# Plain fp32 products in place of split ones in a hyena layer's transforms

## The chip, the cores and the metric

One core of one Trainium2 chip. The metric is the device time of one execution in microseconds; less is better. TensorE is PE, VectorE is DVE, ScalarE is ACT, GpSimd is POOL and SyncE is SP.

## The reference

Two layers over 512 latent tokens of width 1024, with 256 context tokens in the first: attention with an MLP, then a hyena layer with an MLP, all in fp32. The part that matters here is the hyena mixer:

```python
def bidir_long_conv(u, hf, hb, skip):
    L = u.shape[1]
    kfull = jnp.concatenate([hf, jnp.zeros_like(hf[:1]), hb[:0:-1]], axis=0)
    K = jnp.fft.rfft(kfull, n=2 * L, axis=0)
    uf = u.astype(F32)
    U = jnp.fft.rfft(uf, n=2 * L, axis=1)
    y = jnp.fft.irfft(U * K[None], n=2 * L, axis=1)[:, :L]
    return (y + uf * skip.astype(F32)).astype(u.dtype)

def hyena_mixer(h, w_in, conv_w, conv_b, ..., skip, w_out):
    z = short_conv(h @ w_in, conv_w, conv_b)
    x1, x2, v = jnp.split(z, 3, axis=-1)
    hf, hb = hyena_filters(...)
    y = v
    for n, gate in enumerate((x1, x2)):
        y = gate * bidir_long_conv(y, hf[:, n], hb[:, n], skip[n])
    return y @ w_out
```

## The kernel before

PE can take fp32 data in a reduced form, fp32r. To keep the precision of fp32 the kernel writes an operand as a sum of two fp32r tiles, hi (ACT casts) and lo (DVE subtracts, line 172; weights at lines 125 and 126), and makes three products of the halves: hi x hi, hi x lo and lo x hi (`mm3`, lines 107 to 111).

The hyena layer works on four groups of 256 channels, c = 0 to 3. The transforms are products with tables of cosines and sines, Tf (forward) and Ti (back), which `load_tables` brings from DRAM. For each group:

- `conv1(c)` transposes v into u and calls `hyena_conv` with quarter true. There `spectrum` multiplies u by Tf (8 triples), and DVE adds the results (line 938) into tiles named ft0 and ft1, merges them into U (line 926), multiplies by the filter's spectrum K (line 1076, one product of it on POOL), and forms the sums E and O, again in tiles named ft0 and ft1. From these come P0 and P1, split.
- `gate1` multiplies P0 and P1 by Ti (8 triples); DVE multiplies by x1 into y1, which is split into u.
- `hyena_conv` with quarter false makes the second convolution from that u; E and O are split into P0 and P1 as they are. The result is called R2.
- `gate2` uses R2 as the stationary operand and Ti as the moving one (16 triples); DVE multiplies by x2, and y is split for the output projection.

A transform tile has one buffer (bufs=1): u, U, ft0, ft1, P0 and P1 each exist once, and a new tile of a name waits until the last reader of the old one is done. Projections of later groups (and parts of the output projection) are put in between by `fill(n)`, each 24 products of 512 columns on PE, or 6 to 12 for the output. In the program conv1(c + 1) stands right behind the second convolution of c, then come 4, 5 or 9 fills, and then gate2(c). A scheduler orders the instructions of each engine by that priority when it builds the program, and lets a later one go first where an earlier one isn't ready. The order is fixed then.

After the loop the output projection's last part keeps its split weights for both token halves in tiles of the transforms that are no longer needed (`kept`, an alias of names), and the next MLP's first weights are put into others (`wx`).

Of the kernel before, what the change touches and what calls it, by code (L numbers as in the profile page):

```python
# [9 lines left out]
F32 = mybir.dt.float32  # L10
F32R = mybir.dt.float32r
AF = mybir.ActivationFunctionType
ALU = mybir.AluOpType
AX = mybir.AxisListType
P = 128
# [54 lines left out]
class Kernel:  # L70
# [840 lines left out]
    def load_tables(self, pool, inverse):  # L911

        nc, src = self.nc, self.a["k_dft"]
        res = []
        for nm, sl in (("Tf", slice(0, 8)), ("Ti", slice(10, 22))) if inverse else (("Tf", slice(0, 10)),):
            n = sl.stop - sl.start
            t = Split(pool.tile([P, n, P], F32R, name=nm + "hi", bufs=1), pool.tile([P, n, P], F32R, name=nm + "lo", bufs=1))
            nc.gpsimd.dma_start(out=t.hi, in_=src[:, 0, sl])
            nc.gpsimd.dma_start(out=t.lo, in_=src[:, 1, sl])
            res.append(t)  # L920
        return res

    def merge(self, U, E, O, e0, e1):

# [7 lines left out]
    def spectrum(self, T, x, pool, U):  # L932

        nc = self.nc
        V = nc.vector
        tt = lambda o, x, y, op: V.tensor_tensor(out=o, in0=x, in1=y, op=op)
        res = []
        for par in range(2):  # L940
            ps = {}
            for r in (par + 2, par):
                ps[r] = self.sm()
                for i in range(2):
                    self.mm3(ps[r][:, 256 * i:256 * i + 256], T[:, 2 * r + i], x[:, r], True, True)
            b = pool.tile([P, 512], F32, name=("fcb", "fsb")[par], bufs=1)
            nc.scalar.copy(b, ps[par + 2])
            a = ps[par]
            o = pool.tile([P, 2, 512], F32, name=f"ft{par}", bufs=1)
            tt(o[:, 0], a, b, ALU.add)  # L950
            if par == 0:
                tt(o[:, 1], a, b, ALU.subtract)
            else:
                for h in range(2):
                    sl, dl = slice(256 * h, 256 * h + 256), slice(256 - 256 * h, 512 - 256 * h)
                    tt(o[:, 1, dl], a[:, sl], b[:, sl], ALU.subtract)
            res.append((o[:, 0], o[:, 1]))
        self.merge(U, *res, V, V)
# [112 lines left out]
    def hyena_conv(self, hp, T, u, K, quarter):  # L1071


        nc = self.nc
        V, G = nc.vector, nc.gpsimd
        tt = lambda e, o, x, y, op: e.tensor_tensor(out=o, in0=x, in1=y, op=op)  # L1076
        U = hp.tile([P, 8, 256], F32, name="U", bufs=1)
        self.spectrum(T, u, hp, U)
        c, s = slice(0, 4), slice(4, 8)
        t0 = hp.tile([P, 4, 256], F32, name="ft0", bufs=1)  # L1080
        t1 = hp.tile([P, 4, 256], F32, name="ft1", bufs=1)
        tt(G, t1, U[:, c], K[:, s], ALU.mult)
        tt(V, t0, U[:, s], K[:, s], ALU.mult)
        tt(V, U[:, s], U[:, s], K[:, c], ALU.mult)
        tt(V, U[:, c], U[:, c], K[:, c], ALU.mult)
        tt(V, U[:, c], U[:, c], t0, ALU.subtract)
        tt(V, U[:, s], U[:, s], t1, ALU.add)
        E = hp.tile([P, 4, 256], F32, name="ft0", bufs=1)
        O = hp.tile([P, 4, 256], F32, name="ft1", bufs=1)

        tt(V, E, U[:, 0:8:2], U[:, 1:8:2], ALU.add)
        res = []
        for i, X in enumerate((E, O)):
            if i:
                tt(V, O[:, 0:4:2], U[:, 0:8:4], U[:, 1:8:4], ALU.subtract)
                tt(V, O[:, 1], U[:, 7], U[:, 6], ALU.subtract)
                tt(V, O[:, 3], U[:, 2], U[:, 3], ALU.subtract)
            d = Split(hp.tile([P, 4, 256], F32R, name=f"P{i}hi", bufs=1), hp.tile([P, 4, 256], F32R, name=f"P{i}lo", bufs=1))
            if quarter:
                for b, op in enumerate((ALU.add, ALU.subtract)):  # L1100
                    t = hp.tile([P, 2, 256], F32, name="y1", bufs=3)
                    tt(V, t, X[:, 0:4:2], X[:, 1:4:2], op)
                    self.split_to(d[:, 2 * b:2 * b + 2], t)
            else:
                self.split_to(d, X)
            res.append(d)
        return res

    def hyena(self, h, zp, first, open_hp, kdram, gcol, finish):
        nc, a = self.nc, self.a  # L1110
# [39 lines left out]

        def conv1(c):

            u = Split(hp.tile([P, 4, 256], F32R, name="uhi", bufs=1), hp.tile([P, 4, 256], F32R, name="ulo", bufs=1))
            for o, ps in turned(c, "v"):
                self.split_to(u[:, o], ps)
            return self.hyena_conv(hp, Tf, u, load_k(0, c), True)

        def turn_x1(c):
# [4 lines left out]

        def gate1(c, R, x1):

            u = Split(hp.tile([P, 4, 256], F32R, name="uhi", bufs=1), hp.tile([P, 4, 256], F32R, name="ulo", bufs=1))
            for o in range(2):
                ps = self.sm()
                for b in range(2):
                    for i in range(2):  # L1170
                        self.mm3(ps[:, 256 * b:256 * b + 256], Ti[:, 6 * o + 3 * i + b], R[o][:, 2 * b + i], i == 0, i == 1)
                t = hp.tile([P, 2, 256], F32, name="y1", bufs=3)
                nc.vector.tensor_tensor(out=t, in0=ps.rearrange("p (t n) -> p t n", t=2), in1=x1[:, o:4:2], op=ALU.mult)
                self.split_to(u[:, o:4:2], t)
            return u

        def gate2(c, R):

            for m in range(2):
                ps = self.sm().rearrange("p (o b n) -> p o b n", o=2, b=2)  # L1180
                for o in range(2):
                    for n in range(4):
                        i, j = 6 * o + 3 * (n // 2), n % 2
                        self.mm3(ps[:, o], R[o][:, n, m * P:(m + 1) * P], Ti[:, i:i + 2 + j:1 + j], n == 0, n == 3)
                t = hp.tile([P, S], F32, name="y1", bufs=3)
                v = lambda ap: ap.rearrange("p (b o n) -> p o b n", o=2, b=2)
                nc.vector.tensor_tensor(out=v(t), in0=ps, in1=v(Z[c]["x2"][m]), op=ALU.mult)
                s = Split(hp.tile([P, S], F32R, name="yhi", bufs=4), hp.tile([P, S], F32R, name="ylo", bufs=4))
                self.split_to(s, t)
                Y[2 * c + m] = s  # L1190
# [11 lines left out]
        hp = open_hp()  # L1202
        Tf, Ti = self.load_tables(hp, True)
# [7 lines left out]
        for c in range(4):  # L1211
            u = gate1(c, R1, turn_x1(c))
# [8 lines left out]
        fill(99)  # L1221
        kept = [Alias(p, {"whi": (hi, b), "wlo": (lo, b)}) for p, hi, lo, b in (
            (zp, "zv", "zx1", 2), (zp, "zv", "zx1", 2), (hp, "fcb", "fsb", 1), (zp, "zx2", "zx2", 2),
            *((hp, f"{nm}hi", f"{nm}lo", 1) for nm in ("P0", "P1", "Tf")), (hp, "ft0", "ft1", 1))]
        return finish(lambda hf: wo(6, 8, hf, kept))


# [32 lines left out]
    def build(self):  # L1260
        tc, nc, a = self.tc, self.nc, self.a

        pool = lambda **kw: tc.tile_pool(reuse_waits="tile", **kw)
        with ExitStack() as es:
# [41 lines left out]
            op = op_es.enter_context(pool(name="op", bufs=5))  # L1306
# [17 lines left out]
            hp = hp_es.enter_context(pool(name="hp", bufs=1, side="right"))  # L1324
            np_es = E(ExitStack())
            wx = np_es.enter_context(pool(name="wx", bufs=2, side="right"))
# [12 lines left out]
            with pool(name="mlp", bufs=1) as mp:  # L1339
                with ExitStack() as bg_es:  # L1340
                    for g in range(4):
                        H = self.mlp_up(0, h, mp, g, () if g else first)
                        if g == 0:
# [3 lines left out]
                            T, = self.load_tables(fp, False)  # L1347
# [8 lines left out]
                wx = np_es.enter_context(pool(name="wx2", bufs=2, side="right"))  # L1356
# [9 lines left out]
            hy = []  # L1366
# [6 lines left out]
            def finish(proj):  # L1373
                h = self.new_h(hp)
                np_ = Parts(hy[0].tile([P, 8, 256], F32, name="U", bufs=1),
                            Alias(hy[0], {"nxr": ("y1", 3), "nu": ("y1", 3)}),
                            {"nacc": (0, 1), "ny": (2, 3), "nv": (4, 5), "nt": (6,), "nsq": (7, 6)})
                wx = (Alias(hy[0], {"whi": ("uhi", 1), "wlo": ("ulo", 1)}),
                      Alias(hy[0], {"whi": ("x1T", 1), "wlo": ("Kin", 1)}))
                return h, self.project_norm_project(  # L1380
                    proj, lambda hf: self.normT(np_, h, m1[4], m1[3], hf), h,
                    lambda: self.weight(a["mlp_w1"][1][:, 0:256], KD, 256, wx), 3)
# [20 lines left out]
def _r12(x):  # L1403

    u = np.ascontiguousarray(x, np.float32).view(np.uint32).astype(np.uint64)
    u = (u + 0x7FF + ((u >> 12) & 1)) >> 12 << 12
    return u.astype(np.uint32).view(np.float32)


def _tables():  # L1410
    t = {}
# [37 lines left out]
            tabs += [fn(ang(eo)), fn(ang(eo + 2)), -fn(ang(eo + 2))]  # L1449
    m = np.stack(tabs, 1).astype(np.float64)  # L1450
    hi = _r12(m.astype(np.float32))
    t["k_dft"] = np.ascontiguousarray(np.stack([hi, _r12((m - hi).astype(np.float32))], 1))

    tt = np.arange(S, dtype=np.float32)
    tn = tt / np.float32(S)
# [33 lines left out]
```

## Time and profile before

| | |
|---|---|
| median of 3 runs | 1602.5 us (1600.34 to 1606.98) |
| profiled execution, device time | 1603.73 us |
| its span on the core | 1601.9 us |
| PE busy | 1467.2 us, 92% |
| DVE busy | 1151.7 us, 72% |
| ACT busy | 720.7 us, 45% |
| POOL busy | 468.5 us, 29% |
| mean granted clock | 0.964 of 2.4 GHz |

The hyena layer's conv loop lies between about 929 and 1207 us of the span. A busy PE is an engine with a product in flight: the distance between the starts of two products tells what one costs in a row of them, the length of one also holds its way through the array. An idle time is put down to what ended it.

### The profile page before, as it was taken

To read this page: it belongs to the slowest core of one execution; us is meant where nothing else is said; L and a number is where in the kernel's file an instruction comes from. 1 tells how busy PE (TensorE), PEld (TensorE's weight loads), DVE (VectorE), ACT (ScalarE), POOL (GpSimd) and SP (SyncE) were. 2 spreads that over 40 slices of the span, in tenths; PEclk is the share of its full clock that TensorE was granted. 3 is DMA by queue.
4 is the path that set the end of the run, shared out by engine and by line. 5 is a ranking of instruction groups with operands and counts; after the bars stand their busy time and mean duration, and the time that the engine had idled before them with its cause. 6 is when DMAs were issued, how large, how long until landed. Compare 5 with 4: busy or idle time off the path is not lost. (4 is left out here: it accounts for less than half of the span.)

```text
span 1601.9 us, 20203 instructions
## 1 busy us (share of the span) xinstructions
PE 1467.2 (92%) x7628; PEld 1217.3 (76%) x7628; DVE 1151.7 (72%) x1603; ACT 720.7 (45%) x1172; POOL 468.5 (29%) x363
## 2 busy tenths in 40 slices
PE   7689899999899999999999987888798999999998
PEld 2356688888887777877889866777677888888898
DVE  2888899887678898999755668888977534344354
ACT  3534587666654344345334534444235423232242
POOL 0350235222320332323221475666564000000001
PEclk9889899999999999999999998998998999999999
DMA  7556200221356555655334332221313132332341
GB/s 296 200 163 221 55 1 19 58 52 48 119 177 230 178 175 169 205 173 170 99 112 158 114 110 79 79 79 41 105 53 119 53 105 80 105 105 82 102 132 53
DMA packets 134751, 187.40 MB, mean 117 GB/s; under 512 B 16616, under 2 KB 117741, under 8 KB 131582
## 3 DMA queue, kind: packets, MB, share of 16 engines
q1 hardware_dynamic: 131904, 173.31, 33.6%
q0 software_dynamic: 2016, 12.32, 2.3%
q8 instruction: 60, 0.98, 0.3%
q10 hardware_dynamic: 734, 0.48, 0.1%
q14 instruction: 37, 0.30, 0.1%
HBM read 172.98 MB, written 10.49 MB: 115 GB/s over the span
## 5 line engine op out<-in xcount | busy, mean ns | idle before, releaser
L125 ACT CAST whi<-wraw 128x1024 fp32r<-128x1024 f32 (+3 forms) x211 | 198.8, 949 | 374.3 <-PE sm L110 341.4
L126 DVE TENSOR_TENSOR wlo<-wraw,whi 128x1024 fp32r<-128x1024 f32 (+4 forms) x184 | 223.8, 1219 | 129.4 <-ACT whi L125 126.1
L111 PE MATMUL sm<-h_hi,wlo 128*128 128x512 f32 (+1 forms) x720 | 277.7, 387 | 6.5 <-DVE wlo L126 5.5
L109 PE MATMUL sm<-h_hi,whi 128*128 128x512 f32 (+1 forms) x720 | 279.3, 391 | 3.7 <-ACT h_hi L420 2.3
L110 PE MATMUL sm<-h_lo,whi 128*128 128x512 f32 (+1 forms) x720 | 278.4, 387 | 2.9 <-POOL h_lo L424 2.3
L111 PE MATMUL sm<-mHhi,wlo 128*128 128x512 f32 (+1 forms) x640 | 223.1, 349 | 3.1 <-DVE wlo L126 3.1
L109 PE MATMUL sm<-mHhi,whi 128*128 128x512 f32 (+1 forms) x640 | 225.2, 352 | 0.5 <-ACT mHhi L169 0.3
L110 PE MATMUL sm<-mHlo,whi 128*128 128x512 f32 (+1 forms) x640 | 222.9, 348 | 2.5 <-DVE mHlo L172 2.5
L835 DVE SCALAR_TENSOR_TENSOR xT<-sm,mod,xT 128x512 f32<-128x512 f32 (+1 forms) x136 | 83.7, 621 | 138.9 <-PE sm L111 138.9
L111 PEld LDWEIGHTS sm<-h_hi,wlo 128*128 128x128 f32 x720 | 137.9, 192 | 35.8 <-DVE wlo L126 8.5
L110 PEld LDWEIGHTS sm<-h_lo,whi 128*128 128x128 f32 x720 | 138.2, 192 | 31.9 <-POOL h_lo L424 4.6
L109 PEld LDWEIGHTS sm<-h_hi,whi 128*128 128x128 f32 x720 | 138.0, 193 | 32.2 <-issue 3.4
L111 PEld LDWEIGHTS sm<-mHhi,wlo 128*128 128x128 f32 x640 | 121.1, 189 | 19.5 <-DVE wlo L126 4.6
L110 PEld LDWEIGHTS sm<-mHlo,whi 128*128 128x128 f32 x640 | 121.2, 189 | 19.2 <-DVE mHlo L172 3.4
L109 PEld LDWEIGHTS sm<-mHhi,whi 128*128 128x128 f32 x640 | 121.3, 190 | 17.2 <-issue 1.4
L926 POOL TENSOR_TENSOR Kout<-kE,kO 128x512 f32<-128x512 f32 x32 | 52.1, 1654 | 262.9 <-ACT kO L1064 262.9
L1242 POOL TENSOR_TENSOR facc<-facc,fsq 128x256 f32<-128x256 f32 x12 | 9.5, 789 | 333.5 <-ACT fsq L1240 333.5
L639 POOL TENSOR_SCALAR prob<-prob,smx 128x768 f32<-128x768 f32 x64 | 60.1, 939 | 149.1 <-DVE smx L638 95.7
L370 DVE SCALAR_TENSOR_TENSOR modacc<-modw,silu,modacc 128x1024 f32<-128x1024 f32 x63 | 83.8, 1330 | 11.0 <-DMA modw<-in_w_mod 10.6
L169 ACT CAST mHhi<-ms 128x512 fp32r<-128x512 f32 x64 | 39.7, 620 | 83.8 <-DVE ms L875 83.6
L1124 POOL TENSOR_TENSOR zx<-zx,zt 128x384 f32<-128x384 f32 (+1 forms) x64 | 60.4, 964 | 38.2 <-ACT zt L1122 37.0
L637 ACT ACTIVATE prob<-big,smx,qry 128x768 f32<-128x768 f32 x64 | 63.7, 996 | 11.1 <-DVE smx L635 10.4
(500 smaller groups left out, 3319.5 us busy)
## 6 DMA issues: line engine op xcount, KB each, us to landing
wraw<-in_mlp_w SPq DMA_DIRECT2D x67, 1024.0 KB
modw<-in_w_mod SPq DMA_DIRECT2D x80, 512.0 KB
wraw<-in_h_w_in SPq DMA_DIRECT2D x12, 1024.0 KB
wm<-in_w_mod SPq DMA_DIRECT2D x8, 1024.0 KB
kd<-Kout POOLq DMA_DIRECT2D x8, 1024.0 KB, 5.0
Kin<-kd SPq DMA_DIRECT2D x8, 1024.0 KB
wraw<-in_a_w_in SPq DMA_DIRECT2D x5, 1024.0 KB
wraw<-in_a_w_out SPq DMA_DIRECT2D x9, 512.0 KB
```

What stands on the lines that cost most here:

```text
L109: mm(ps, w.hi, x.hi, start=first, stop=False)
L110: mm(ps, w.hi, x.lo, start=False, stop=False)
L111: mm(ps, w.lo, x.hi, start=False, stop=last)
L125: nc.scalar.copy(hi, r3)
L126: (lo_eng or nc.vector).tensor_tensor(out=lo, in0=r3, in1=f(hi), op=ALU.subtract)
L169: nc.scalar.copy(dst.hi, src)
L370: nc.vector.scalar_tensor_tensor(out=acc, in0=w, scalar=s, in1=acc, op0=ALU.mult, op1=ALU.add)
L637: nc.scalar.activation(out=p, in_=sf, func=AF.Exp, bias=sm[:, 1:2], scale=sc, accum_out=sm[:, 2:3])
L639: nc.gpsimd.tensor_scalar(out=p, in0=p, scalar1=sm[:, 3:4], scalar2=1.0, op0=ALU.mult, op1=ALU.mult)
L835: nc.vector.scalar_tensor_tensor(out=xt, in0=ps, scalar=gcol[:, d:d + 1], in1=xt, op0=ALU.mult, op1=ALU.add)
L926: tt = lambda e, o, x, y, op: e.tensor_tensor(out=o, in0=x, in1=y, op=op)
L1124: nc.gpsimd.tensor_tensor(out=t[:, o0:o0 + n], in0=t[:, o0:o0 + n], in1=b[:, i0:i0 + n], op=ALU.add)
```

## The change

The transforms of the hyena layer's convolutions no longer use split operands. The table gets a third, unsplit copy in DRAM; `load_tables(pool, True)` loads Tf and Ti from it as fp32 on SP's queue, while the filter's tables stay split and on POOL's. `spectrum`, `gate1` and `gate2` make one fp32 product where `mm3` made three. u is a copy, or DVE's product itself; with quarter true P0 and P1 are written by DVE's sums; with quarter false `hyena_conv` returns E and O themselves. The kept weights and the next weights get other tiles, kw0 to kw3 and wl among them, since P0lo, P1lo, Tflo and ulo are gone.

```diff
@@ load_tables
-        for nm, sl in (("Tf", slice(0, 8)), ("Ti", slice(10, 22))) if inverse else (("Tf", slice(0, 10)),):
-            n = sl.stop - sl.start
-            t = Split(pool.tile([P, n, P], F32R, name=nm + "hi", bufs=1), pool.tile([P, n, P], F32R, name=nm + "lo", bufs=1))
-            nc.gpsimd.dma_start(out=t.hi, in_=src[:, 0, sl])
-            nc.gpsimd.dma_start(out=t.lo, in_=src[:, 1, sl])
-            res.append(t)
-        return res
+        if inverse:
+            for nm, sl in (("Tf", slice(0, 8)), ("Ti", slice(10, 22))):
+                t = pool.tile([P, sl.stop - sl.start, P], F32, name=nm, bufs=1)
+                nc.sync.dma_start(out=t, in_=src[:, 2, sl])
+                res.append(t)
+            return res
...
@@ spectrum
-                    self.mm3(ps[r][:, 256 * i:256 * i + 256], T[:, 2 * r + i], x[:, r], True, True)
+                    nc.tensor.matmul(ps[r][:, 256 * i:256 * i + 256], T[:, 2 * r + i], x[:, r], start=True, stop=True)
@@ hyena_conv
-            d = Split(hp.tile([P, 4, 256], F32R, name=f"P{i}hi", bufs=1), hp.tile([P, 4, 256], F32R, name=f"P{i}lo", bufs=1))
             if quarter:
+                d = hp.tile([P, 4, 256], F32, name=f"P{i}", bufs=1)
                 for b, op in enumerate((ALU.add, ALU.subtract)):
-                    t = hp.tile([P, 2, 256], F32, name="y1", bufs=3)
-                    tt(V, t, X[:, 0:4:2], X[:, 1:4:2], op)
-                    self.split_to(d[:, 2 * b:2 * b + 2], t)
-            else:
-                self.split_to(d, X)
-            res.append(d)
+                    tt(V, d[:, 2 * b:2 * b + 2], X[:, 0:4:2], X[:, 1:4:2], op)
+                X = d
+            res.append(X)
@@ conv1
-            u = Split(hp.tile([P, 4, 256], F32R, name="uhi", bufs=1), hp.tile([P, 4, 256], F32R, name="ulo", bufs=1))
+            u = hp.tile([P, 4, 256], F32, name="u", bufs=1)
             for o, ps in turned(c, "v"):
-                self.split_to(u[:, o], ps)
+                nc.scalar.copy(u[:, o], ps)
@@ gate1
-            u = Split(hp.tile([P, 4, 256], F32R, name="uhi", bufs=1), hp.tile([P, 4, 256], F32R, name="ulo", bufs=1))
+            u = hp.tile([P, 4, 256], F32, name="u", bufs=1)
...
-                        self.mm3(ps[:, 256 * b:256 * b + 256], Ti[:, 6 * o + 3 * i + b], R[o][:, 2 * b + i], i == 0, i == 1)
-                t = hp.tile([P, 2, 256], F32, name="y1", bufs=3)
-                nc.vector.tensor_tensor(out=t, in0=ps.rearrange("p (t n) -> p t n", t=2), in1=x1[:, o:4:2], op=ALU.mult)
-                self.split_to(u[:, o:4:2], t)
+                        nc.tensor.matmul(ps[:, 256 * b:256 * b + 256], Ti[:, 6 * o + 3 * i + b], R[o][:, 2 * b + i],
+                                         start=(i == 0), stop=(i == 1))
+                nc.vector.tensor_tensor(out=u[:, o:4:2], in0=ps.rearrange("p (t n) -> p t n", t=2), in1=x1[:, o:4:2], op=ALU.mult)
@@ gate2
-                        self.mm3(ps[:, o], R[o][:, n, m * P:(m + 1) * P], Ti[:, i:i + 2 + j:1 + j], n == 0, n == 3)
+                        nc.tensor.matmul(ps[:, o], R[o][:, n, m * P:(m + 1) * P], Ti[:, i:i + 2 + j:1 + j],
+                                         start=(n == 0), stop=(n == 3))
@@ hyena
-            *((hp, f"{nm}hi", f"{nm}lo", 1) for nm in ("P0", "P1", "Tf")), (hp, "ft0", "ft1", 1))]
+            (hp, "P0", "P1", 1), (hp, "kw0", "kw1", 1), (hp, "kw2", "kw3", 1), (hp, "ft0", "ft1", 1))]
@@ finish
-                wx = (Alias(hy[0], {"whi": ("uhi", 1), "wlo": ("ulo", 1)}),
+                wx = (Alias(hy[0], {"whi": ("u", 1), "wlo": ("wl", 1)}),
@@ _tables
-    t["k_dft"] = np.ascontiguousarray(np.stack([hi, _r12((m - hi).astype(np.float32))], 1))
+    t["k_dft"] = np.ascontiguousarray(np.stack([hi, _r12((m - hi).astype(np.float32)), m.astype(np.float32)], 1))
```

## Rows read from the trace of the kernel before

**Rows 1.** Busy (x count) by stretch: length, PE, PEld, DVE, ACT, POOL; clock, DMA.

```profile
929.00:1019.30 90.30, 73.67 (x362) 63.20 (x361) 73.90 (x71) 37.08 (x55) 57.34 (x41) 0.87 0.24 83
...
1000.30:1019.30 19.00, 19.00 (x103) 16.55 (x102) 16.61 (x16) 9.33 (x13) 13.86 (x10) 0.94 0.17 56
1019.30:1064.60 45.30, 35.62 (x181) 30.16 (x180) 40.96 (x45) 18.65 (x30) 27.51 (x20) 0.92 0.27 93
1064.60:1091.30 26.70, 25.22 (x128) 21.21 (x127) 24.27 (x22) 11.39 (x16) 21.23 (x15) 0.95 0.23 79
1091.30:1129.10 37.80, 28.61 (x146) 24.76 (x145) 31.77 (x39) 15.21 (x26) 20.02 (x15) 0.86 0.13 42
1129.10:1156.70 27.60, 21.89 (x113) 18.15 (x111) 24.12 (x28) 9.77 (x17) 16.66 (x13) 0.94 0.36 115
1156.70:1198.30 41.60, 37.57 (x190) 31.40 (x190) 33.40 (x42) 15.53 (x27) 22.53 (x18) 1.00 0.17 51
```

**Rows 2.** PE's waits from 929 to 1207.1: us in total, times, longest.

```profile
PE sm L110 <- DVE ulo L172: 12.1, 4, 4.0
PE sm L109 <- ACT uhi L169: 6.9, 4, 2.8
PE sm L109 <- ACT P0hi L169: 6.3, 3, 2.6
PE sm L109 <- ACT P1hi L169: 5.9, 2, 4.1
PE sm L110 <- DVE P0lo L172: 5.7, 3, 4.5
```

**Rows 3.** Timeline of PE around L405: start, length, instruction.

```profile
905.61 0.28 PE L111 MATMUL sm<-h_hi,wlo 128*128 128x256 f32 x1
905.73 0.59 PE L405 MATMUL sm<-nacc,ones 128*128 128x256 f32 x2
906.16 0.59 PE L406 MATMUL sm<-nsq,ones 128*128 128x256 f32 x2
...
906.71 0.28 PE L110 MATMUL sm<-h_lo,whi 128*128 128x256 f32 x1
```

**Rows 4.** Busy time of line 172, of line 169, and group ylo, 929 to 1211.

```profile
929.00:1211.00 282.00, 39.53 (x48) 0.00 (x0) 0.91 0.23 76
...
929.00:1211.00 282.00, 32.07 (x48) 0.91 0.23 76
...
L172 DVE TENSOR_TENSOR ylo<-y,yhi 128x512 fp32r<-128x512 f32 x8 | 7.2, 927 | 1.6 <-ACT yhi L169 1.6
```

**Rows 5.** Timeline of DVE: the second spectral sums and a first spectrum sum.

```profile
996.85 3.44 DVE L1076 TENSOR_TENSOR ft<-U 128x1024 f32<-128x1024 f32 x4
...
1001.53 0.69 DVE L938 TENSOR_TENSOR ft<-sm,fcb 128x512 f32<-128x512 f32 x1
...
1061.18 3.43 DVE L1076 TENSOR_TENSOR ft<-U 128x1024 f32<-128x1024 f32 x4
...
1126.64 2.48 DVE L1076 TENSOR_TENSOR ft<-U 128x1024 f32<-128x1024 f32 x4
...
1195.84 2.48 DVE L1076 TENSOR_TENSOR ft<-U 128x1024 f32<-128x1024 f32 x4
```

**Rows 6.** gate2's products with Tilo by group: min/median/max ns, first and last start.

```profile
L110 PE MATMUL sm<-Tilo,P1hi x8: 283/284/284, 1009.9 to 1018.9; 128*128 128x256 f32 x8
...
L110 PE MATMUL sm<-Tilo,P1hi x8: 283/284/284, 1087.0 to 1090.9; 128*128 128x256 f32 x8
...
L110 PE MATMUL sm<-Tilo,P1hi x8: 274/284/416, 1148.5 to 1156.3; 128*128 128x256 f32 x8
...
L110 PE MATMUL sm<-Tilo,P1hi x8: 284/350/416, 1201.1 to 1206.7; 128*128 128x256 f32 x8
```

**Rows 7.** The chain that ended last, behind the last gate2: start, length.

```profile
1207.05 0.41 ACT P1hi L125
...
1208.99 6.07 DMA wraw<-in_mlp_w
```

More of the change, by code (lines that the diff above doesn't have):

```diff
@@ L914, in load_tables @@
         res = []
-        for nm, sl in (("Tf", slice(0, 8)), ("Ti", slice(10, 22))) if inverse else (("Tf", slice(0, 10)),):
-            n = sl.stop - sl.start
-            t = Split(pool.tile([P, n, P], F32R, name=nm + "hi", bufs=1), pool.tile([P, n, P], F32R, name=nm + "lo", bufs=1))
-            nc.gpsimd.dma_start(out=t.hi, in_=src[:, 0, sl])
-            nc.gpsimd.dma_start(out=t.lo, in_=src[:, 1, sl])
-            res.append(t)
-        return res
+        if inverse:
[4 more added lines that the diff above has]
+            return res
+        t = Split(pool.tile([P, 10, P], F32R, name="Tfhi", bufs=1), pool.tile([P, 10, P], F32R, name="Tflo", bufs=1))
+        nc.gpsimd.dma_start(out=t.hi, in_=src[:, 0, 0:10])
+        nc.gpsimd.dma_start(out=t.lo, in_=src[:, 1, 0:10])
+        return [t]
     def merge(self, U, E, O, e0, e1):
```

## The prediction

> **What bounds the kernel now.** I began with the page: PE is the busiest engine by far, so a change to products is priced on PE first. But the change touches only the hyena layer, whose conv loop is the dip of PE in the page's slices, so the next view is busy time by stretch, cut where each channel group's second inverse transform (gate2) ends and where its second spectral sums are ready [rows 1]. There PE is busy 73.7 + 35.6 + 25.2 + 28.6 + 21.9 + 37.6 us of 90.3 + 45.3 + 26.7 + 37.8 + 27.6 + 41.6: between 929 and 1198.3 us it is idle 46.7 us, and DVE, busy 228 us of 269, is as loaded as PE. This layer is a chain between the two. PE's waits there are nearly all for the halves of split operands: 12.1 us for ulo, 6.9 for uhi, 6.3 for P0hi, 5.9 for P1hi and 5.7 for P0lo [rows 2]. The reader is to see that the layer is bound by order, not by one engine. Outside the layer nothing changes.
>
> The timeline of DVE gives the chain's marks. The second spectral sums of group 0 end at 1000.3, of group 1 at 1064.6, of group 2 at 1129.1, of group 3 at 1198.3 (start plus length of the four sums), and the next group's first spectrum sum starts 1.2 us after the first of them, at 1001.53 [rows 5]. gate2, which reads those sums, ends on PE later: 1019.3, 1091.3, 1156.7, 1207.1 (last start of Tilo x P1 plus the following products) [rows 6]. So today the next conv1 runs on DVE for 19.0, 26.7 and 27.6 us while gate2 waits its turn on PE, behind projections which stand before it in the program: in those stretches PE is busy 19.0 of 19.0, 25.2 of 26.7 and 21.9 of 27.6 [rows 1].
>
> **Products.** An fp32r product of 256 columns starts 0.12 us after the one before (905.61 to 905.73), so a split triple takes 0.36. A plain fp32 product of the same shape is on the trace: the sums over partitions at L405 and L406. Each is two instructions, and the pair takes 0.43 (905.73 to 906.16); the fp32r product after L406 again gets its place 0.43 later, 0.12 before 906.71 [rows 3]. The layer has 64 spectrum, 32 gate1 and 64 gate2 triples, 160 of 256 columns: 160 x (0.43 - 0.36) = **11.2 us more PE work**, 2.8 per group. PE gets no cheaper by this change. The row fits streaming: 0.43 is four times 256 columns at 2.4 GHz, while the fp32r product's 0.12 is more than 256 / 2.4 = 0.107. The Trainium skill (FP8 and Floating Point Precision, "TensorE Precision Notes") says that true FP32 is four passes through the array against one in the reduced form; by that alone the ratio is 4/3 and the addition 160 x 0.12 = 19 us, an estimate. The row gives less, since fp32r at this width is not held by its columns, and the row decides.
>
> **Removed splits.** The subtractions of line 172 take 39.5 us of DVE in the layer, 7.2 of them for y, which stays: 32.3 go. Line 169 takes 32.1 us of ACT; the cast of y stays, u from PSUM becomes a plain copy of the same size, the rest goes, some two thirds [rows 4]. DVE gains 8 us per group. In the chain to the first spectral sums (1000.3 today) this is worth: about 2.3 us at the first spectrum (ulo is one of PE's waits there, but the slower spectrum follows), 2.6 for the P halves, 1.3 for u after gate1, 1.3 for the next u's halves that were slipped in: **7.5 us, so 992.8** [rows 4, 5].
>
> **Moved: a wait that appears.** With quarter false the sums are no longer copied into P0/P1; gate2 reads E and O themselves, which are the tiles ft0 and ft1 with one buffer each. The next conv1's first spectrum sums are written to ft0 and ft1 too. So this DVE work, now at 1001.53 for group 1, must wait until gate2 of the group before has ended. Behind it on DVE stands the whole next conv1, and gate1, conv2 follow. The overlap of 19 to 27 us seen above is gone. I sum the layer along that chain:
>
> - 992.8 for the first sums.
> - From a gate2's end to the next sums: today first sum to last is 1001.53 to 1064.6, 63.1 us. Out of it go the halves of R2's P1 (1.2), P (2.6), u after gate1 (1.3), the next u (1.4) and some 1.2 of ACT casts between; the wider products add 0.9; some weight subtractions move into the wait (2). That leaves 55, and 57 for the third, which has residual updates in it [rows 4, 5].
> - gate2 itself after the last sums: 16 products, 7.2.
> - Total 992.8 + 55 + 55 + 57 + 7.2 = 1167, plus the three waits d0 + d1 + d2. Today's last gate2 ends at 1207.1, so the change is neutral at d0 + d1 + d2 = **40 us**; today the three are 73 [rows 5, 6].
>
> The waits are set by what PE has left to do. d0: up to the first gate2's end PE has 73.7 us of work and 16.6 idle [rows 1]; the work grows by 3.4, the idle halves, as half of it was for lo halves: 1019.3 + 3.4 - 8.5 = 1014, d0 = 21. d1: 35.6 + 25.2 + 2.9 = 63.7 of work, plus 6 idle (11.2 today), less 55 under the chain: 15. d2: 28.6 + 21.9 + 2.9 = 53.4, plus 9 idle (14.9 today), less 55: 7.4. Sum 43, **3 us later** than today. The longer chain lets PE do its projections under it, so these waits shrink, but the last group has little left to fill (37.6 of 41.6 today, then some 40 of 57).
>
> **Smaller edits.** The tables are two loads of 1.3 MB together on SP's queue, where there were four of 2.6 MB on POOL's. Behind them on SP stand the layer's weight loads; the nearest row has a load of 1 MB on that queue at 6.07 us [rows 7], so weights could come up to 8 us later, of which the second weight buffer hides most: I take nothing, 3 us at worst. POOL loses four issues, off the path. In the tail the kept weights no longer reuse P1 and Tf: today the cast into P1 waits for gate2's end (1207.05), frees the raw weight, whose next load takes 6.07 us and holds ACT ahead of the next norm [rows 7]. With own tiles that starts earlier: 0 to 3.5, I take **2 us** gained. The larger table in DRAM costs nothing.
>
> Sum against the profiled execution: span 1601.9, device time 1603.7; 1603.7 + 3 - 2 = 1605. The median of the runs is 1602.5, 1.2 lower, so I say **1603**: no change that can be measured.
>
> **Rivals.** *The gain stays.* The waits on ft0 and ft1 cost nothing because gate2 slips into PE's gaps early, so that d0 + d1 + d2 is near 3 x 7.2. Then PE bounds up to 1198.3: 222.6 us of work, 10 more for the products, and 46.7 of idle less 27 (all of ulo and P0lo, half of the three hi waits), together 252 in place of 269: **17 us faster, 1585**. For it: those waits are the largest on PE [rows 2], and DVE loses 8 us per group. Against it: PE is busy through all three waits with work that stands earlier in the program [rows 1].
>
> *Slower.* The held ft0 and ft1 stop the next conv1 while PE clears projections, and under the chain PE does no more of them than today, because their weights are split late on DVE and POOL. Then the waits stay near 57, that is 40 + 17: **1620**. It decides at a sum of 48 (40 + 8). For it: PE is idle 9.7 us of 45.3 and 9.2 of 37.8 in the chain stretches today although projections are left [rows 1]. Against it: the removed 8 us per group on DVE make those splits earlier.
>
> *Dearer or cheaper products.* If a plain product took the place of four fp32r products, 4 x 0.12 = 0.48, PE would work another 160 x 0.05 = 8 us: 1611. If the plain product were run in one instruction at fp32r's 0.12 the change would save 160 x 0.24 = 38 us, 1565; L405 speaks against both [rows 3].
>
> **How the numbers follow.** About 0.5% (8 us) is what a measurement of this kernel can tell from no change. Chances: forecast 0.43, gain stays 0.26, slower 0.26, products 0.05 (0.04 dearer, 0.01 cheaper). Range 1585 to 1622: the first two rivals at their prices, 2 us of chain above the slower one, leaving out the one-pass case, waits as long as today's, and the outer half of each rival. Faster 0.27, same 0.43, slower 0.30; the dearer product lies at the edge and goes to slower.
>
> **What would show it.** Products: pairs at 0.43 in the spectrum, PE work in the layer up by 11 us; 0.48 would make the dearer rival right. Splits: no rows of line 172 but ylo and what remains of the filters, and no wait of PE for ulo. The wait: DVE's first spectrum sum of a group starts only after gate2 of the group before, with DVE idle ahead of it, released by PE; if conv1 still starts right after the sums, I misread the buffers. Chain: about 55 us from gate2's end to the next sums. The waits: 21, 15 and 7. If their sum is under 32 the kernel is faster, over 48 slower. The forecast falls most easily with d1 and d2, which rest on how PE's work is ordered, and the trace of before can't show the new order.

## The result, and the profile after

The kernel after takes 1613.3 us (median of 12 runs, 1606.16 to 1615.87) where the kernel before takes 1602.6 in the same comparison (12 runs, 1595.41 to 1608.66): a ratio of 1.0057, 95% interval 1.0039 to 1.0075. It is slower by 0.57%, some 10.7 us. The forecast was 1603 us and no change that can be measured.

I begin with busy time by stretch, cut at the layer's first and last mark on PE: the end of the first transposes of `zv`, and the end of the last gate2. The columns are start, end and length, then the busy time of PE, PEld, DVE, ACT and POOL, the granted clock, the DMA share and GB/s. Of the kernel before:

```profile
0.00:930.03 930.03, 858.44 (x4540) 696.60 (x4540) 731.77 (x1099) 477.42 (x800) 269.26 (x206) 0.97 0.43 139
930.03:1207.07 277.04, 229.32 (x1149) 195.35 (x1150) 234.49 (x246) 109.02 (x173) 168.55 (x122) 0.91 0.22 74
1207.07:1601.90 394.83, 379.42 (x1941) 325.34 (x1939) 185.42 (x258) 134.24 (x201) 30.70 (x36) 0.98 0.30 94
```

And of the kernel after:

```profile
0.00:922.33 922.33, 858.07 (x4540) 696.19 (x4540) 729.85 (x1099) 477.23 (x800) 268.43 (x201) 0.97 0.44 140
922.33:1210.45 288.12, 229.37 (x990) 190.13 (x990) 195.94 (x206) 89.09 (x142) 162.50 (x124) 0.91 0.21 70
1210.45:1604.40 393.95, 377.50 (x1940) 323.38 (x1939) 185.87 (x258) 134.02 (x201) 30.05 (x35) 0.98 0.29 94
```

The layer grew from 277.0 to 288.1 us, the tail (what follows it) shrank by 0.9. Together that is 10.2, nearly all of the 10.7. The two spans alone, 1601.9 and 1604.4, hide this: the profiled run of after is the fastest of its runs and reached the layer 7.7 us earlier with the same work (PE 858.4 and 858.1 us there), and no run here shows why. Within the layer DVE lost 38.6 us and ACT 19.9, and PE is as busy as before. So the 11 us are idle time of PE.

The marks of the chain, in the kernel after: PE's timeline (start, length, instruction) with a spectrum and the four gate2s, then DVE's with the four second spectral sums, the first spectrum sums of the next group, and what DVE did ahead of one of them (in brackets the idle time before an instruction, and who ended it).

```profile
968.36 3.62 PE L948 MATMUL sm<-u,Tf 128*128 128x256 f32 x16
...
998.92 7.07 PE L1183 MATMUL sm<-Ti,ft 128*128 128x256 f32 x32
...
1071.96 7.07 PE L1183 MATMUL sm<-Ti,ft 128*128 128x256 f32 x32
...
1143.19 7.07 PE L1183 MATMUL sm<-Ti,ft 128*128 128x256 f32 x32
...
1203.30 7.15 PE L1183 MATMUL sm<-Ti,ft 128*128 128x256 f32 x32 [2.22 <-DVE ft L1079]
```

```profile
984.89 6.50 DVE L1079 TENSOR_TENSOR ft<-U 128x1024 f32<-128x1024 f32 x4
...
1004.62 1.28 DVE L941 TENSOR_TENSOR ft<-sm,fcb 128x512 f32<-128x512 f32 x2
...
1052.50 6.49 DVE L1079 TENSOR_TENSOR ft<-U 128x1024 f32<-128x1024 f32 x4
...
1067.58 1.43 DVE L126 TENSOR_TENSOR wlo<-wraw,whi 128x1024 fp32r<-128x1024 f32 x1 [7.24 <-ACT whi L125]
1075.68 0.69 DVE L1187 TENSOR_TENSOR y<-sm,zx 128x512 f32<-128x512 f32 x1 [6.68 <-PE sm L1183]
1077.06 0.69 DVE L172 TENSOR_TENSOR ylo<-y,yhi 128x512 fp32r<-128x512 f32 x1 [0.68 <-ACT yhi L169]
1077.67 1.28 DVE L941 TENSOR_TENSOR ft<-sm,fcb 128x512 f32<-128x512 f32 x2
...
1126.13 2.59 DVE L1079 TENSOR_TENSOR ft<-U 128x1024 f32<-128x1024 f32 x4
...
1200.83 3.59 DVE L1079 TENSOR_TENSOR ft<-U 128x1024 f32<-128x1024 f32 x4
```

The reader is to see the new wait. Before, the next group's first spectrum sum started right behind the last group's sums, at 1001.53 where the four end at 1000.3 [rows 5]. Now DVE's sums of group 1 end at 1059.0, gate2 of that group ends on PE at 1079.03, and the first spectrum sum of group 2 starts at 1077.67, as gate2 nears its end. In between DVE stood idle for 7.24 and 6.68 us. From sums to gate2's end the three waits are 14.6, 20.0 and 21.5 us. PE's waits in the layer (us in total, times, longest):

```profile
PE sm L1171 <- DVE P L1079: 43.8, 5, 16.2
PE sm L948 <- ACT u L1155: 7.0, 4, 3.4
PE sm L111 <- POOL wlo L126: 3.0, 2, 2.0
```

All waits for halves of transform operands [rows 2] are gone. In their place PE stands 43.8 us in five waits at gate1 (L1171) for P, which the end of conv1 writes. Two of the five, 5.0 us together, stand at group 0, ahead of any hold; the other three, 12.9, 16.2 and 9.6 us, wait for a conv1 that the held tiles delay. Here is a stretch by stretch view of the same kernel, cut at the marks. The last four rows are gate1's products of groups 1, 2 and 3 and one spectrum by themselves:

```profile
991.40:1005.99 14.59, 14.59 (x67) 12.46 (x66) 5.32 (x6) 7.18 (x10) 13.34 (x14) 1.00 0.44 144
1005.99:1059.00 53.01, 39.37 (x175) 32.74 (x175) 41.55 (x44) 15.85 (x24) 25.96 (x16) 0.87 0.17 60
1059.00:1079.03 20.03, 20.03 (x92) 16.91 (x92) 5.35 (x6) 8.23 (x11) 15.24 (x15) 1.00 0.20 65
1079.03:1128.70 49.67, 31.25 (x138) 26.03 (x137) 35.26 (x43) 12.04 (x21) 20.29 (x15) 0.83 0.14 48
1128.70:1150.25 21.55, 19.58 (x81) 16.09 (x80) 9.88 (x13) 6.87 (x13) 10.20 (x12) 0.92 0.35 107
...
1025.23:1030.67 5.44, 5.44 (x17) 4.49 (x18) 3.12 (x6) 0.00 (x0) 0.00 (x0) 0.67 0.01 3
1096.13:1101.96 5.83, 5.83 (x17) 4.81 (x18) 3.11 (x6) 0.00 (x0) 0.00 (x0) 0.63 0.00 0
1171.65:1177.26 5.61, 5.61 (x17) 4.67 (x18) 4.12 (x6) 0.00 (x0) 1.52 (x2) 0.65 0.01 3
968.36:971.98 3.62, 3.62 (x19) 3.16 (x18) 1.49 (x2) 3.62 (x6) 1.27 (x2) 1.00 0.07 9
```

DVE and PE now take turns. In the waits PE is full (20.03 of 20.03) and DVE nearly empty (5.35); under the chain DVE works (41.55 of 53.01) and PE idles 13.6 and 18.4 us. The idling costs a second time: after waits of 12.9, 16.2 and 9.6 us gate1's 16 instructions ran at a mean granted clock of 0.63 to 0.67, so partly at 1.2 and partly at 2.4 GHz. They took 5.44, 5.83 and 5.61 us, where the spectrum's 16 took 3.62 at a granted clock of 1.00.

### The profile page after: what moved, and what is told of

The parts are those of the page before. It is cut to its first block, busy times and chain, and to the rows that moved or that the text cites. A ratio compares the mean times of both kernels' runs of the same rounds, so it can differ in the third digit from the quotient of the medians.

```text
span 1604.4 us, 19790 instructions
## 1 busy us (share of the span) xinstructions
PE 1464.9 (91%) x7468; PEld 1209.7 (75%) x7468; DVE 1111.7 (69%) x1563; ACT 700.3 (44%) x1140; POOL 461.0 (29%) x359
## 5 line engine op out<-in xcount | busy, mean ns | idle before, releaser
L835 DVE SCALAR_TENSOR_TENSOR xT<-sm,mod,xT 128x512 f32<-128x512 f32 (+1 forms) x136 | 83.7, 621 | 149.8 <-PE sm L111 149.8
L111 PEld LDWEIGHTS sm<-mHhi,wlo 128*128 128x128 f32 x640 | 121.2, 189 | 19.9 <-DVE wlo L126 4.7
L1124 POOL TENSOR_TENSOR zx<-zx,zt 128x384 f32<-128x384 f32 x64 | 68.1, 1086 | 56.0 <-ACT zt L1122 54.7
L637 ACT ACTIVATE prob<-big,smx,qry 128x768 f32<-128x768 f32 x64 | 63.7, 996 | 11.5 <-DVE smx L635 10.9
```

Source lines behind the costliest of these rows:

```text
L111: mm(ps, w.lo, x.hi, start=False, stop=last)
L637: nc.scalar.activation(out=p, in_=sf, func=AF.Exp, bias=sm[:, 1:2], scale=sc, accum_out=sm[:, 2:3])
L835: nc.vector.scalar_tensor_tensor(out=xt, in0=ps, scalar=gcol[:, d:d + 1], in1=xt, op0=ALU.mult, op1=ALU.add)
L1124: nc.gpsimd.tensor_tensor(out=t[:, o0:o0 + n], in0=t[:, o0:o0 + n], in1=b[:, i0:i0 + n], op=ALU.add)
```

## The experiments

My theory after the result: the second sums held in `ft0` and `ft1` cost more than the removed splits bring, and the wider products cost their price on top. Rivals: the products alone make it slower; it is the order in which gate2 stands; or PE is held by the projections' own weight halves. All times are medians, all ratios against the kernel before, run beside each; a layer's length is from the one profiled run.

**e1_own.** The sums get tiles of their own.

```
-        E = hp.tile([P, 4, 256], F32, name="ft0", bufs=1)
-        O = hp.tile([P, 4, 256], F32, name="ft1", bufs=1)
+        E = hp.tile([P, 4, 256], F32, name="ft0" if quarter else "R20", bufs=1)
+        O = hp.tile([P, 4, 256], F32, name="ft1" if quarter else "R21", bufs=1)
```

> The changed kernel, but the second convolution's E and O (R2) get tiles of their own, R20 and R21, so that the next conv1 need not wait for gate2; the products stay plain fp32. Theory (the wait on ft0 and ft1 is what costs): the overlap of conv1 with gate2's wait comes back, the layer falls from 288 us to 255-265, the kernel to 1580-1592, below the kernel before; DVE's first spectrum sum starts within 2 us of the second spectral sums. Rival (dearer products cost it: 11 us more PE work, and the order doesn't matter): the kernel stays at 1608-1616.

Measured: 1596.2 us, ratio 0.9965 [0.9946, 0.9984]; the layer (from the same marks) 269.0 us. Nothing but two tile names turns the kernel after from 0.57% slower into 0.35% faster: 15 us by the ratios, 17 by the medians. The next conv1 starts right behind the sums again, as in the timeline of DVE:

```profile
983.57 6.60 DVE L1079 TENSOR_TENSOR R<-U 128x256 f32<-128x256 f32 x4
990.10 1.27 DVE L941 TENSOR_TENSOR ft<-sm,fcb 128x512 f32<-128x512 f32 x2
```

PE's waits, and POOL's timeline around the longest of them, which ends on PE at 1124.48:

```profile
PE sm L111 <- POOL wlo L126: 15.3, 3, 12.6
PE sm L111 <- DVE wlo L126: 7.3, 2, 3.9
PE sm L948 <- ACT u L1155: 7.2, 4, 3.4
PE sm L1171 <- DVE P L1079: 5.0, 2, 4.8
```

```profile
1113.76 3.38 POOL L1079 TENSOR_TENSOR ft<-U,Kin 128x1024 f32<-128x1024 f32 x1 [4.05 <-DVE U L929]
1117.10 5.66 POOL L1124 TENSOR_TENSOR zx<-zx,zt 128x384 f32<-128x384 f32 x4
1122.73 2.39 POOL L126 TENSOR_TENSOR wlo<-wraw,whi 128x256 fp32r<-128x256 f32 x2
```

The wait for P falls from 43.8 to 5.0 us. What is late next is a weight half of the output projection, queued on POOL behind a filter product and shifted sums: 12.6 us in one wait. POOL wasn't busy throughout: it stood idle for 4.05 us ahead of that filter product, which waited for DVE. I hadn't expected this wait, and I take it to be what holds the time above the expected 1592; no run shows that, as the three below that try to remove it get slower.

**e2_p.** The same with other tiles: the sums go to `P0` and `P1`, which are free then, so no memory is added.

```
+        E = hp.tile([P, 4, 256], F32, name="ft0" if quarter else "P0", bufs=1)
+        O = hp.tile([P, 4, 256], F32, name="ft1" if quarter else "P1", bufs=1)
```

> The changed kernel, but R2's E and O are written into P0 and P1, as the kernel before had R2's halves in P0 and P1: the next conv1 runs up to its own P and only there waits for gate2. Theory (the wait's place costs): nearly all of e1_own's gain, within 6 us of it, since gate2 ended before conv1 reached P in the kernel before. Rival (any hold by gate2 costs the same, wherever it stands): it stays with the changed kernel, 1608-1616.

Measured: 1595.4 us, 0.9957 [0.9937, 0.9977], layer 273.0 in the one profiled run: the same time as e1_own within the intervals. It isn't more memory that helps, but that the next conv1's first sums go to tiles that gate2 doesn't hold; only its last ones, into P0 and P1, must come behind gate2.

**e3_gate2first.** The other way to shorten the wait: gate2 ahead of the next conv1 and of the projections.

```
-            fill((0, 0, 1, 2)[c])
+            fill((2, 2, 2, 2)[c])
+            gate2(c, R2)
             if c < 3:
                 R1 = conv1(c + 1)
-            fill((4, 5, 9, 4)[c])
-            gate2(c, R2)
-            fill((1, 0, 2, 1)[c])
+            fill((3, 3, 10, 5)[c])
```

> The changed kernel with its shared ft0 and ft1, but gate2 stands in the program ahead of the next conv1 and of all projections except the two that make x2. Theory (the wait is long because gate2 stands behind 4, 5 and 9 projections on PE): the three waits d0+d1+d2 fall from 56 us to about 25, the chain from the first sums to the last gate2 falls by 20-30 us, and PE becomes the bound: 1585-1597. Rival (the waits are PE's own work and come back as idle PE later in the loop): 1605-1616.

Measured: 1632.1 us, 1.0177 [1.0152, 1.0202]. My expectation fell. gate2 came early, and PE then waited for the sums themselves:

```profile
PE sm L1183 <- DVE ft L1079: 31.3, 4, 10.4
PE sm L1171 <- DVE P L1079: 18.5, 7, 4.8
```

What I had called a wait was PE's own projections, and with gate2 ahead of them they were not done earlier either: each kind of projected tile has two buffers, which I take to be why, though that wasn't tried. The layer is 293.9 us and what follows it 405.9, where the kernel after has 288.1 and 394.0: PE's idle time in the layer grew from 58.8 to 66.0 us, and 12 of the 18 us by which the two together grew are products that now stand behind the loop (11.3 us more PE work there). So moving gate2 forward didn't remove the cost; part of it became a wait of PE, and this edit alone can't say how much of the rest is the moved work.

**e4_before_hold.** The hold without the plain products: the kernel before, with the hi halves of the second sums in `ft0` and `ft1`. The sums themselves, which had been there, go to `x1T` and a tile of their own, by two more lines that aren't shown.

```
+            d = Split(hp.tile([P, 4, 256], F32R, name=f"P{i}hi" if quarter else f"ft{i}", bufs=1),
+                      hp.tile([P, 4, 256], F32R, name=f"P{i}lo", bufs=1))
```

> The kernel before, split products and all, with the hold alone: the hi halves of R2 are put into ft0 and ft1, so that the next conv1 waits for gate2 as in the changed kernel; E is made in x1T and O in a tile of its own in its place. Theory: slower than the kernel before by 15-30 us, 1617-1632, with DVE idle ahead of the first spectrum sums. Rival (the hold is harmless, the products cost the 10 us): within 5 us of the kernel before.

Measured: 1631.4 us, 1.0167 [1.0138, 1.0195]. PE's waits:

```profile
PE sm L109 <- ACT P0hi L169: 38.6, 4, 16.3
PE sm L110 <- DVE ulo L172: 15.0, 4, 5.4
```

The hold alone costs 27 us by the ratio, 30 by the medians, on split products, with the same wait at gate1 (longest 16.3, in the kernel after 16.2). So a hold alone is enough for a loss; what the reuse of `x1T` adds to it wasn't run by itself. The kernel after lies some 18 us below this one (1.0167 less 1.0057). That isn't what the rest of the change is worth without a hold: e1_own is only some 6 us below the kernel before.

**e7_own_three and e8_own_one.** What the products themselves cost: e1_own with single fp32r operands and three equal fp32r products in each place, or one. Both leave out the low halves, and both load the tables on POOL's queue.

```
+    def mmr(self, ps, w, x, first, last):
+        for n in range(3):
+            self.nc.tensor.matmul(ps, w, x, start=first and n == 0, stop=last and n == 2)
```

> e1_own, but every operand of the transforms is one fp32r tile and every product is three equal fp32r products, which takes PE 0.36 us in place of 0.43; the lo halves and so part of each product are left out, and the tables come on POOL's queue. It has the split kernel's PE work without its splits. Theory (the dearer product is paid where PE is the bound, in the waits for gate2, but is partly hidden under the chain): faster than e1_own by 4-11 us. Rival (PE's idle time swallows it): within 4 us of e1_own.

> As e7_own_three, with one fp32r product where there were three: two thirds of each product are left out, 0.12 us of PE in place of 0.43, some 50 us less PE work in the layer. Theory (the layer is a chain of DVE, ACT and POOL steps with PE work under it): the kernel falls by much less than 50 us against e1_own, 15-30 us. Rival (PE is the bound of the layer once the hold is gone): 40-50 us.

Measured: 1583.3 us, 0.9881 [0.9848, 0.9915], and 1580.1 us, 0.9866 [0.983, 0.9901]. The layers by themselves, three products and one:

```profile
926.73:1181.58 254.85, 218.53 (x1149) 188.56 (x1150) 203.91 (x206) 89.16 (x143) 168.95 (x125) 0.93 0.23 79
```

```profile
929.22:1180.66 251.44, 195.35 (x829) 158.42 (x830) 206.27 (x203) 87.53 (x140) 163.64 (x123) 0.86 0.24 79
```

In e1_own PE is busy 228.9 us there with 990 instructions (I read it from the same view). Three reduced products in place of a plain one take 10.4 us off PE and 13 off the time, more than the 4 to 11 that I expected: with the hold gone the wider product seems to be paid. The next 23 us of PE's work bring 2 to 3, within the intervals of the two: there PE waits 19.1 us for P and 11.6 for u, so I take the chain to be the bound. I can't say how much of the 13 us is due to order: the POOL wait of 12.6 us in e1_own is 7.7 in e7_own_three.

**e6_own_dve, e11_own_alt and e9_before_dve.** Three tries at the late weight halves: the output projection's low halves on DVE in place of POOL, in e1_own and in the kernel before, and every second one in e1_own.

```
-            w_out, list(range(r0, r1)), gcol, lambda k: Y[r0 + k], cols, kept, (nc.gpsimd, nc.gpsimd))
+            w_out, list(range(r0, r1)), gcol, lambda k: Y[r0 + k], cols, kept, (nc.vector, nc.vector))
```

> e1_own with one more edit: the lo halves of the output projection's weights are subtracted on DVE instead of POOL. In e1_own PE waited 12.6 us in one piece for such a half, which stood on POOL behind the filter product and short-convolution sums. Theory (DVE's freed time is not yet used, and POOL's order holds PE): that wait goes, the kernel comes to 1582-1592, below e1_own. Rival (the next in line is as late, or DVE's chain pays for it): within 4 us of e1_own.

> The kernel after with own tiles for the second sums, and of the output projection's weights each second low half on DVE in place of POOL. With all of them on POOL the longest wait of PE is one of 12.6 us for such a half, with all on DVE there are 29.6 us of waits for them. Theory, that it is the place in the two queues that decides and no engine is free of it: half of them on each gives waits for low halves of 12 to 25 us in sum and a time between the two, 1597 to 1604. Rival, that POOL was only overloaded: the sum falls below 10 us and the time to 1586 to 1592.

> The kernel before with the edit of e6_own_dve alone (lo halves of the output projection's weights on DVE). Theory (there DVE is the loaded engine and has no room): same as the kernel before or slower, 1600-1610. Rival (the edit gains on its own, whatever the products): faster than the kernel before by 5 us or more.

Measured: 1605.1 us, 1.0019 [1.0002, 1.0037] for e6_own_dve; 1609.0, 1.0034 [1.0013, 1.0056] for e11_own_alt; 1613.1, 1.0073 [1.0049, 1.0098] for e9_before_dve. All three lie above the kernels that they were made from by 9 to 12 us by the ratios, and above what I expected. PE's waits in e6_own_dve, in e11_own_alt, then in e9_before_dve:

```profile
PE sm L111 <- DVE wlo L126: 29.6, 6, 8.4
```

```profile
PE sm L111 <- DVE wlo L126: 20.0, 5, 7.0
PE sm L111 <- POOL wlo L126: 11.3, 3, 7.7
```

```profile
PE sm L111 <- DVE wlo L126: 24.8, 5, 14.9
```

PE's waits for low halves from either queue come to 22.6 us in e1_own (15.3 and 7.3), 32.6 in e6_own_dve (with 3.0 from POOL) and 31.3 in e11_own_alt; in the kernel before they are 5.6, in e9_before_dve 25.6 (with 0.8 from POOL). So the half comes late in either queue: on POOL behind a filter product and shifted sums, on DVE, as I take it, behind the chain. That POOL was only overloaded is refuted, as half the load on each brought more waits than POOL's share alone. e1_own and e2_p stay the best of the full kernels.

**e10_after_nosums.** The kernel after without most of the shifted sums on POOL, for a thing seen in the marks: four sums that took 3.44 and 3.43 us before [rows 5] take 6.50 and 6.49.

```
-                    nc.gpsimd.tensor_tensor(out=t[:, o0:o0 + n], in0=t[:, o0:o0 + n], in1=b[:, i0:i0 + n], op=ALU.add)
+                    if n < 130:
+                        nc.gpsimd.tensor_tensor(out=t[:, o0:o0 + 1], in0=t[:, o0:o0 + 1], in1=b[:, i0:i0 + 1], op=ALU.add)
```

> The kernel after, of whose short convolution's shifted sums on POOL (L1124) the two 384 wide ones of each tile are left out and the other two cut to one element, so the filter is not computed in full. In the kernel after the four second spectral sums take 6.50 and 6.49 us on DVE in groups 0 and 1, while POOL runs L1124, where the kernel before has 3.44 and 3.43. Theory, that DVE runs slower beside a busy POOL: with L1124 gone the four sums take 2.5 us in both groups, the first of them are ready some 4 us earlier, 65 us after the layer's start in place of 69.1, and the layer is 274 to 282 us in place of 288. Rival, that the sums are slower for another reason (their inputs come late, or their form): they stay near 6.5 us and the layer near 288. The held tiles are still there, so in neither case does the time fall to that with own tiles: 1598 to 1607 by the theory, 1610 to 1615 by the rival.

Measured: 1594.5 us, 0.9954 [0.9929, 0.9978], layer 273.6. The sums:

```profile
979.69 4.58 DVE L1079 TENSOR_TENSOR ft<-U 128x1024 f32<-128x1024 f32 x4
```

They got shorter, but not 2.5: POOL was still at a weight half and two of the cut sums. The time fell further than either theory said, from 1613 to 1594.5, I think because the shifted sums also stand in the chain (the next gate reads their tiles), so this run doesn't price the slowed sums alone. The wait for P is still 35.0 us in four, so the hold is still there. The reader should see that the hold isn't the only lever: with it in place, leaving out work on POOL brought 16 us by the ratios, about what the tile names bring.

## Where the prediction was right and where it was wrong, step by step

The mechanism was right, and so was the side on which it decides: I wrote that over 48 us of waits the kernel is slower, and they are 56.2. The forecast of 43 was the step that failed, and in it the idle time that I left to PE in the periods of groups 1 and 2. The range, 1585 to 1622, holds the time; the largest chance, 0.43, stood on no change, and 0.30 on slower.

From the layer's start the terms compare so (start 930.03 before, 922.33 after):

- **First sums:** forecast 62.8 us (992.8 less 930.03), measured 69.1 (991.4 less 922.33), 70.3 before. Of the 7.5 us of splits only 1.2 came off. The second spectrum didn't follow gate1: it starts at 968.36, behind a projection of 24 products that PE runs from 961.6, so I take the removed halves of u to have been hidden there. And the four sums took 3 us longer. Not seen: PE's queue at that place. **+6.3.**
- **Chains from a gate2's end to the next sums:** forecast 55, 55 and 57, measured 53.0, 49.7 and 54.2. The terms that I listed for 55 add up to 54.3. **-10.2.**
- **Waits:** forecast 21, 15 and 7.4, measured 14.6, 20.0 and 21.5. **+13.2.** I had let PE's idle time shrink to 6 and 9 us in the periods of groups 1 and 2; it is 13.6 and 20.4 (the unfilled parts of the stretches above). PE's work was even a little less than I summed (59.4 and 50.8 us against 63.7 and 53.4). What I missed is where the idling comes from: gate1 of the next group stands on PE ahead of the remaining projections, and PE stops there for P. This is the rival *slower*: it named the idle time, though it put it down to late weight splits, and those are 3.0 us in the kernel after.
- **Last gate2:** forecast 7.2, measured 6.0. **-1.2.**

The sum is +8.1 on a forecast of +3: the layer's 11. The tail gave 0.9 where I took 2.

The first three terms are tied to each other. PE is full in the first two waits, so there PE decides when gate2 ends, and sums that come earlier or later only change the length of the wait. The first gate2 ended 83.7 us after the layer's start, where I had 84: the late first sums cost nothing here. From gate2 to gate2 I had 70 and 62.4 us and the trace shows 73.0 and 71.2, because PE idled 19.0 us more than I allowed and worked 6.9 less. These two periods are 11.9 us over; the last chain and the last gate2 gave 4 back. That the time fell inside the range is owed to the range's width and not to the sum.

**Products.** 0.43 for the pair was right: 16 instructions in 3.62 us, 32 in 7.07, and e7_own_three shows 10.4 us of PE for 160 of them against my 11.2. Yet the test I named, 11 us more PE work in the layer, failed: 229.3 and 229.4. Counted on the trace from each product's start to the next one's, or to its own end, the transforms take 73.8 us before and 77.0 after, and the projections 149.0 and 145.4. So a triple had cost 0.46 and not 0.36, the plain product costs 0.48 and not 0.43, and the projections, the same number in both, gave back the 3 us between. I take the broken triples, in pieces between waits for the halves [rows 2] and partly at the low clock (means of 0.86 to 0.92 in the stretches with idling [rows 1]), to be why; no run shows it alone. *Dearer or cheaper products* is refuted by the 0.43.

**Removed splits.** Right in size: DVE less by 38.6 us in the layer (29.7 in e1_own), where I had 32.3 from the halves alone. They pay when the hold is gone, as e1_own and e2_p show: some 6 us faster than before, in spite of the products. *The gain stays* (1585) asked for that and for 11 us more; it failed on the hold. Without the hold it still lacks 11 us, with 22.6 us of PE's waits for weight halves in e1_own, and no run here brings them back.

**Tables:** No wait of PE is put down to a table; one of 2.7 us ahead of the first gate1 has no releaser in the profile, and what it was stays open.

## What to carry to other kernels

When an edit lets a consumer read an operand where it lies instead of a copy, ask who writes that buffer next and how late the consumer is: here the copy was what set the buffer free, and a tile name was worth 15 to 17 us. Price a new wait by the period of the queue that ends it, its work plus the places at which it will itself stop for the delayed chain, not by its work plus a part of today's idling. And an engine that is waited for isn't always overloaded: in all three kernels in which weight halves went from POOL to DVE, PE's waits for them grew.

## What the runs showed of the hardware that I had not expected

DVE's sums have no length of their own beside a busy POOL. The same four spectral sums take 2.49 us in e6_own_dve, where POOL's timeline is empty around them, and 6.50 in the kernel after:

```profile
1189.33 2.49 DVE L1079 TENSOR_TENSOR R<-U 128x256 f32<-128x256 f32 x4
```

The single sums show where the time goes. These are one sum of 1024 columns and POOL's instruction beside it, in the kernel after and in the kernel before:

```profile
984.89 3.31 DVE L1079 TENSOR_TENSOR ft<-U 128x1024 f32<-128x1024 f32 x1
983.70 3.42 POOL L126 TENSOR_TENSOR wlo<-wraw,whi 128x1024 fp32r<-128x1024 f32 x1 [3.51 <-ACT whi L125]
...
996.85 1.95 DVE L1076 TENSOR_TENSOR ft<-U 128x1024 f32<-128x1024 f32 x1
996.72 1.00 POOL L1124 TENSOR_TENSOR zx<-zx,zt 128x384 f32<-128x384 f32 x1
```

Beside an idle POOL such a sum takes 1.21 us (in the kernel before, at 1126.64). Here it ends 1.08 us after POOL's instruction has ended, in both kernels (988.20 less 987.12, and 998.80 less 997.72), however long that one was: DVE gets next to nothing done until POOL is through. The Trainium skill (SBUF — State Buffer, "SBUF: two separate sides") says that VectorE with two inputs from SBUF and GpSimd lock a shared pair of ports against each other for whole instructions; the two pairs of rows agree with that.

So the largest single loss in the kernel after, 2.1 of the 4.0 us, stands beside a weight half and not beside the shifted sums. e10_after_nosums tests both sides. It keeps the weight half there, and the first sum again takes 3.31 us and ends 1.08 after it; most of the shifted sums are gone, and the other three take 1.35 us, as beside an idle POOL, where the kernel after has 3.26:

```profile
982.92 1.35 DVE L1079 TENSOR_TENSOR ft<-U 128x512 f32<-128x512 f32 x3
...
988.12 3.26 DVE L1079 TENSOR_TENSOR ft<-U 128x512 f32<-128x512 f32 x3
```

So a removed DVE instruction can come back as a longer neighbour, if it moves what is left beside POOL's work.
